# A bidirectional encoder on one core: the last two tiles of the attention branch's gate projection are queued behind the value matmuls of the last attention head

## The chip, the core and the metric

The kernel runs on one core of a Trainium2 chip. The metric is the time of one execution on the device in microseconds; lower is better. A core has engines that run side by side, each working through its own queue in order: the TensorE (PE in the profile; its weight loads are listed as PEld) for matmuls, the VectorE (DVE) for elementwise work and reductions, the ScalarE (ACT) for activation functions and casts, GpSimd (POOL), and SyncE (SP), which here issues the loads. Matmuls write to PSUM, everything else lies in SBUF.

## The reference

Two layers on 512 tokens of width 1024. Each layer normalizes its input, makes ten projections of it with one wide weight matrix `w_in`, runs two token mixers on them side by side (differential attention, and a gated linear recurrence in two directions), projects each mixer's output back to the model's width, gates both per channel and adds them, and projects the sum once more. Then follows a SwiGLU block.

```
h = rmsnorm(x, attn_norm[layer])
proj = h @ w_in[layer]
(a_q, a_k, a_v, b_q, b_ff, b_fb, b_i, b_g, gate_a, gate_b) = split_columns(proj)
y_a = diff_attention(a_q, a_k, a_v, ...) @ w_a[layer]        # 4 heads, values 128 wide
y_b = hgrn2_bidirectional(b_q, b_ff, b_fb, b_i, b_g, ...) @ w_b[layer]
merged = sigmoid(gate_a) * y_a + sigmoid(gate_b) * y_b
x = x + merged @ w_o[layer]
h = rmsnorm(x, ffn_norm[layer])
x = x + (silu(h @ w_gate[layer]) * (h @ w_up[layer])) @ w_down[layer]
```

In `diff_attention` each head has two softmax maps; the weights are the first less lambda times the second, and each head's output is normalized before it is joined with the others.

## The kernel before

**Numbers in two halves.** To keep the precision of float32, each operand of a large matmul is split into a rounded `hi` part and a rest `lo`, and each product is made of three matmuls (`mm3`: hi x hi, hi x lo, lo x hi), all adding into one PSUM bank. The rest `lo` x `lo` is left out. A split is one cast on ACT (the line of `ACT.copy` in `split_act`, L92) and one subtraction on DVE (recorded at L81).

**Projections.** `project_fm` (L214) makes a projection tile by tile. A tile is 128 output channels x 512 tokens. For each tile the weights are split (`wsplit`), then come 3 matmuls for each of the `k` chunks of the contraction (k = 8 for `w_in` and `w_o`, 24 matmuls; k = 4 for `w_a` and `w_b`, 12 matmuls), each with a 128x128 stationary weight block and 512 columns of the normalized input (`hh`, `hl`), then `evac`, which takes the bank to SBUF. Raw weights are loaded 1 MB at a time, which is two tiles with k = 8 and four with k = 4, into a pool of two buffers (`raw`). The split weights lie in a pool with three buffers for `hi` and three for `lo` (L102); a tile's buffers come free when its last matmul that reads them has ended. The accumulators take PSUM banks from a pool of four (`m`); the attention's small work has another four (`s`).

**Order.** The code is written for a framework that queues the instructions at build time. It keeps a priority by the order of the program text: at each point an engine gets the earliest instruction in the text that is ready in the framework's own reckoning. Loads, weight splits and evacuations stand in `with urgent():` blocks, which puts them ahead of everything that isn't urgent. So matmuls that come later in the text fill the places where earlier ones aren't ready. The order that comes out is fixed in each engine's queue. `behind(ins, other)` (L94) adds an edge of order alone: `ins` is queued after `other`, with no semaphore of its own.

**The mixer of one layer, from L726.** The recurrence's projections and its four heads come first. Then, from L790: the value projection; `attention` (L629); the second half of the gate of branch b (`gate_b(4)`, four tiles); the projection of branch b with `w_b`, eight tiles; the gate of branch a, eight tiles in two groups of four (columns from `G_A`, into `ga`), with a sigmoid of three ACT operations for each; then `w_a`, eight tiles (L815), and `w_o` (L821). `w_a` has the four heads as its four chunks, so every tile needs the output `oah`, `oal` of all heads, the last head in its last three matmuls. Its evacuation `merge` multiplies by `ga` and adds to `gb`.

**The attention.** For each of four heads `h` and each of four query blocks `t`: `exps` makes the scores (`qk`, four matmuls, L664 and L667), their negated row maximum (DVE, L669) and the exponentials with their row sums (ACT); `weights` joins the two maps on DVE (L674 to L677) into `e`; four transposes (`wt`, L714) turn them and `split_act` stores them as `wh` and `wl`. The loop is pipelined: the scores of the next block are made before the transposes of this one. When all four blocks of a head are turned, `values` (L679) multiplies them with the values: 12 matmuls into the bank `ao` (L210 to L212, L684 to L686). `finish` (L691) squares `ao`, sums the squares over the channels with two matmuls (`hss`, L406 and L409), scales, and splits the result into `oah` and `oal`. For the last head nothing of the attention follows, so its `values` and `finish` (L719) stand by themselves.

Of the kernel before, what the change touches and what calls it, by code (L numbers as in the profile page):

```python
# [18 lines left out]
P = 128  # L19
D = 1024  # L20
DC = D // P
T = 512
TC = T // P
LAYERS = 2
HEADS = 4
# [22 lines left out]
def kernel(  # L48
# [45 lines left out]
    def behind(ins, other):  # L94

        tc.add_manual_dep(ins.ins, other.ins.name,
                          mybir.DependencyInfo(mybir.DependencyClass.NoSync, mybir.DependencyReason.DATA),
                          reason="keep the tensor engine from waiting")
# [108 lines left out]
        return w[k0 * P:(k0 + nk) * P, c0:c0 + n].rearrange("(k p) c -> p k c", p=P)  # L207

    def mm3(ps, lh, ll, rh, rl, start, stop):
        PE.matmul(ps, lh, rh, start=start, stop=False)  # L210
        PE.matmul(ps, lh, rl, start=False, stop=False)  # L211
        PE.matmul(ps, ll, rh, start=False, stop=stop)  # L212

    def project_fm(w, cols, evac, k=DC, ah=None, al=None):  # L214

        ah = hh if ah is None else ah
        al = hl if al is None else al
        width = 2048 // k
        i = 0
        while i < len(cols):  # L220
            n = 1
            parts = ready.pop(cols[i], None)
            if parts is None:
                while n * P < width and i + n < len(cols) and cols[i + n] == cols[i] + n * P:
                    n += 1
                with urgent():
                    raw = wload(rows(w, 0, k, cols[i], n * P))
            for j in range(n):
                with urgent():
                    wh, wl = parts or wsplit(raw[:, :, j * P:(j + 1) * P])  # L230
                ps = mbank()
                for c in range(k):
                    mm3(ps, wh[:, c, :], wl[:, c, :], ah[:, c, :], al[:, c, :], c == 0, c == k - 1)
                with urgent():
                    evac(i + j, ps)
            i += n
# [157 lines left out]
    def head_squares(ps):  # L394
        sq = sm.tile([P, T], F32, tag="sq", name="hsq")
        act(sq, ps, AF.Square)
        sh = sm.tile([P, T], F32R, tag="sqh", name="sqh", bufs=1)
        sl = sm.tile([P, T], F32R, tag="sql", name="sql", bufs=1)
        first = ACT.copy(sh, sq)
        tt(sl, sq, sh.bitcast(F32), ALU.subtract)  # L400
        return (ps, sq, sh, sl), first
# [227 lines left out]
    def attention(l, aq, ak, avh, avl, oh, ol, ap):  # L629

        def operands(h):

            half = [slice(0, 64), slice(64, 128)]
            turned = []
            for src in (aq, ak):
                pt = bank("qkt")
                for t in range(TC):
                    PE.transpose(pt[:, t * P:(t + 1) * P], src[:, t, h * P:(h + 1) * P], ident)  # L640
                turned.append(pt)
            q2 = ap.tile([P, 2, T], F32R, tag="q2", name="q2", bufs=1)
            ka = ap.tile([P, 2, T], F32R, tag="ka", name="ka", bufs=1)
            kb = ap.tile([P, 2, T], F32R, tag="kb", name="kb", bufs=1)
            for pt, dst, swapped in ((turned[0], q2, None), (turned[1], ka, kb)):
                for c in range(2):
                    own, other = half[c], half[1 - c]
                    hi = dst[own, c, :]
                    ACT.copy(hi, pt[own, :])
                    mark = tt(dst[other, c, :], pt[own, :], hi.bitcast(F32), ALU.subtract)  # L650
                    if swapped is not None:
                        ACT.copy(swapped[other, c, :], pt[own, :])
                        mark = tt(swapped[own, c, :], pt[own, :], hi.bitcast(F32), ALU.subtract)
            return (q2, ka, kb), mark

        def exps(q2, ka, kb, t, mark):

            tok = slice(t * P, (t + 1) * P)
            nm = sm.tile([P, 2], F32, tag="nm", name="nm")
            den = sm.tile([P, 2], F32, tag="den", name="den")  # L660
            e = ap.tile([P, 2, T], F32, tag="e", name="e", bufs=2)
            ps = [bank("qk") for c in range(2)]
            for c in range(2):
                mm = PE.matmul(ps[c], q2[:, c, tok], ka[:, c, :], start=True, stop=False)  # L664
                if t == 0 and c == 0:
                    behind(mm, mark)
                PE.matmul(ps[c], q2[:, c, tok], kb[:, c, :], start=False, stop=True)  # L667
            for c in range(2):
                DVE.tensor_reduce(nm[:, c:c + 1], ps[c], AX.X, ALU.max, negate=True)  # L669
                mark = act(e[:, c, :], ps[c], AF.Exp, bias=nm[:, c:c + 1], accum=den[:, c:c + 1])  # L670
            return e, den, mark

        def weights(e, den):
            DVE.reciprocal(den, den)  # L674
            tt(den, den, dcoef[:, l, :], ALU.mult)
            tsc(e[:, 1, :], e[:, 1, :], den[:, 1:2], None, ALU.mult)
            return stt(e[:, 0, :], e[:, 0, :], den[:, 0:1], e[:, 1, :], ALU.mult, ALU.add)  # L677

        def values(h, wh, wl, mark):  # L679
            po = bank("ao")  # L680
            hc = slice(h * P, (h + 1) * P)
            for s in range(TC):
                if s == 0 and mark is not None:
                    behind(PE.matmul(po, avh[:, s, hc], wh[:, s, :], start=True, stop=False), mark)  # L684
                    PE.matmul(po, avh[:, s, hc], wl[:, s, :], start=False, stop=False)
                    PE.matmul(po, avl[:, s, hc], wh[:, s, :], start=False, stop=False)  # L686
                else:
                    mm3(po, avh[:, s, hc], avl[:, s, hc], wh[:, s, :], wl[:, s, :], s == 0, s == TC - 1)
            return head_squares(po)[0]

        def finish(h, parts, mark):  # L691
            o = head_norm(*parts, dgain[:, 4 * l + h:4 * l + h + 1], mark)
            split_act(o, oh[:, h, :], ol[:, h, :])

        todo = [(h, t) for h in range(HEADS) for t in range(TC)]
        ops, mark = operands(0)
        e, den, _ = exps(*ops, 0, mark)
        for n, (h, t) in enumerate(todo):
            mark = weights(e, den)
            if t == 0:  # L700
                if h:
                    parts = values(h - 1, wh, wl, mark)
                wh = ap.tile([P, TC, T], F32R, tag="wh", name="wh", bufs=1)
                wl = ap.tile([P, TC, T], F32R, tag="wl", name="wl", bufs=1)
            elif t == 1 and h:
                finish(h - 1, parts, mark)
            w, mark = e, None
            if n + 1 < len(todo):
                if t == TC - 1:
                    ops, mark = operands(h + 1)  # L710
                e, den, mark = exps(*ops, todo[n + 1][1], mark)
            pt = bank("wt")
            for s in range(TC):
                tr = PE.transpose(pt[:, s * P:(s + 1) * P], w[:, 0, s * P:(s + 1) * P], ident)  # L714
                if mark is not None:
                    behind(tr, mark)
            tok = slice(t * P, (t + 1) * P)
            split_act(pt.rearrange("p (s c) -> p s c", c=P), wh[:, :, tok], wl[:, :, tok])
        finish(HEADS - 1, values(HEADS - 1, wh, wl, None), None)  # L719


    last_silu = None
    for l in range(LAYERS):
        win = w_in[l]
        an = [vecs[:, V_FFN + 8 * l + c:V_FFN + 8 * l + c + 1] for c in range(DC)]
        with ExitStack() as mix:  # L726
# [10 lines left out]
            def scaled(dst):  # L737

                return lambda i, ps: tt(dst(i), ps, rbc, ALU.mult)
# [40 lines left out]
            with tc.tile_pool(name=f"merge{l}", bufs=1, reuse_waits="tile") as gm, ExitStack() as late:  # L780
# [11 lines left out]
                with tc.tile_pool(name=f"attn{l}", bufs=1, reuse_waits="tile") as ap:  # L792
                    rope(aq, ap)
                    rope(ak, ap)
                    attention(l, aq, ak, avh, avl, oah, oal, ap)
                    gate_b(4)
                    project_fm(w_b[l], [i * P for i in range(DC)],
                               lambda i, ps: tt(gb[:, i, :], gb[:, i, :], ps, ALU.mult),
                               k=4, ah=obh, al=obl)
                    ga = [gp.tile([P, HEADS, T], F32, tag=tag, name="ga") for tag in ("obh", "obl")]  # L800
                    for j in range(2):
                        project_fm(win, [G_A + (4 * j + i) * P for i in range(4)], scaled(lambda i: ga[j][:, i, :]))
                        for i in range(4):
                            sigmoid(ga[j][:, i, :])
                mp = late.enter_context(tc.tile_pool(name=f"mrg{l}", bufs=1, reuse_waits="tile"))
# [144 lines left out]
```

## Time and profile before

| what | value |
|---|---|
| median of three runs | 1627.63 us (1626.99 to 1627.94) |
| profiled execution | 1627.93 us |
| its span, first to last instruction | 1626.2 us |
| mean granted TensorE clock | 0.999 |
| PE busy | 1604.3 us, 99% of the span |
| PEld busy | 1323.7 us, 81% |
| DVE busy | 1010.8 us, 62% |
| ACT busy | 776.6 us, 48% |
| mean DMA traffic | 88 GB/s |

Rows of the profile's page and of the timeline name the line, the engine, the operation, and what is written and read by the program's own names (`m<-hh,hi`: a bank `m` from `hh` and `hi`). In the timeline the first two columns are the start from the beginning of the span and the duration, both in us; a bracket at the end gives the idle time of the engine ahead of the row and the instruction whose end released it. In the rows of a waits list stand the total in us, how many times, and the longest. A matmul's recorded duration holds a part that overlaps the next one, so it is the distance between starts that tells the rate. Because helpers record every call under one line, L210 to L212 are the three matmuls of every `mm3`, L81 is every DVE operation with two tensors, and L92 every cast of a split; the names tell them apart. `m<-hh` and `m<-hl` are projections of the layer's input, `m<-obh` is `w_b`, `m<-oah` and `m<-oal` are `w_a`, `m<-mh` and `m<-ml` are `w_o`. (In some rows the operands of a matmul are listed by the stationary one last.)

### The profile page before, as it was taken

The page shows a single profiled execution, that of the slowest core. Times are in us where ns is not written, and L with a number is a line of the kernel's source. Part 1 is how long each engine was busy: PE and PEld are TensorE (multiplying, and loading weights), DVE is VectorE, ACT ScalarE, POOL GpSimd, SP SyncE. Part 2 cuts the span into 40 slices and gives each one's busy share as a digit, 9 for nine tenths or more (in the row PEclk, how much of TensorE's full clock was granted, in tenths as well). Part 3 has the DMA queues.
Part 4 walks back from the last instruction along what each step waited for, and adds up shares of the span by engine and source line. Part 5 has one row for each costly group of instructions (what it writes and reads, how often), then busy time and mean ns, then how long its engine had stood idle before and what let it go on. Part 6 is the DMA issues. An engine that isn't in the chain of part 4 may idle for free.

```text
span 1626.2 us, 18701 instructions
## 1 busy us (share of the span) xinstructions
PE 1604.3 (99%) x7456; PEld 1323.7 (81%) x7456; DVE 1010.8 (62%) x1626; ACT 776.6 (48%) x1192; POOL 7.8 (0%) x21
## 2 busy tenths in 40 slices
PE   8999999999999999999999999999999999999998
PEld 6788888887888888888888888888878888888886
DVE  7878967887644444433368789788876444444224
ACT  5666675676433232322255567676754323233213
POOL 1000000000000000000000000000000000000000
PEclk9999999999999999999999999999999999999999
DMA  5212212221322233322332222122122233332321
GB/s 188 91 65 78 78 53 78 78 78 33 123 91 91 84 98 104 104 91 98 97 104 78 78 78 66 65 71 85 52 79 89 93 104 104 104 99 96 104 83 73
DMA packets 118823, 142.53 MB, mean 88 GB/s; under 512 B 3024, under 2 KB 101328, under 8 KB 118736
## 3 DMA queue, kind: packets, MB, share of 16 engines
q1 hardware_dynamic: 118592, 141.31, 26.8%
q8 instruction: 58, 0.95, 0.2%
q14 instruction: 29, 0.24, 0.0%
q10 hardware_dynamic: 144, 0.03, 0.0%
HBM read 139.23 MB, written 2.10 MB: 87 GB/s over the span
## 4 chain that ended last, share of the span: by engine, by line
PE 85%; DVE 9%; ACT 4%; issue 1%; DMA 0%; SPq 0%; ACTq 0%
PE m L210 24%; PE m L212 24%; PE m L211 24%; DVE fl L81 2%; DVE lo L81 2%; PE sc L551 2%; PE s L212 1%; PE s L211 1%; PE s L210 1%; PE qk L667 1%; DVE z L81 1%; PE wt L714 1%; PE po L601 1%; PE qk L664 1%; ACT hi L92 1%
## 5 line engine op out<-in xcount | busy, mean ns | idle before, releaser
L92 ACT CAST hi<-raw 128x1024 fp32r<-128x1024 f32 (+2 forms) x280 | 276.6, 989 | 612.2 <-PE m L211 469.5
L210 PE MATMUL m<-hh,hi 128*128 128x512 f32 x1216 | 476.7, 392 | 7.1 <-ACT hh L78 7.1
L211 PE MATMUL m<-hl,hi 128*128 128x512 f32 x1216 | 476.1, 392 | 0.1
L212 PE MATMUL m<-hh,lo 128*128 128x512 f32 x1216 | 476.2, 392 | 0.0
L81 DVE TENSOR_TENSOR lo<-raw,hi 128x1024 fp32r<-128x1024 f32 (+2 forms) x280 | 320.3, 1145 | 184.8 <-ACT hi L92 183.6
L210 PEld LDWEIGHTS m<-hh,hi 128*128 128x128 f32 x1216 | 229.2, 188 | 54.6 <-ACT hh L78 7.9
L211 PEld LDWEIGHTS m<-hl,hi 128*128 128x128 f32 x1216 | 228.9, 188 | 48.0 <-DVE hl L84 1.4
L212 PEld LDWEIGHTS m<-hh,lo 128*128 128x128 f32 x1216 | 229.1, 188 | 47.1
L81 DVE TENSOR_TENSOR gu<-m,rbc 128x512 f32<-128x512 f32 x88 | 60.9, 692 | 241.0 <-PE m L212 237.0
L210 PE MATMUL m<-hi,hh 128*128 128x512 f32 x256 | 101.5, 396 | 0.0
L211 PE MATMUL m<-lo,hh 128*128 128x512 f32 x256 | 100.9, 394 | 0.0
L212 PE MATMUL m<-hi,hl 128*128 128x512 f32 x256 | 100.8, 394 | 0.0
L78 ACT ACTIVATE fl<-fl 128x1024 f32<-128x1024 f32 (+1 forms) x56 | 48.4, 872 | 43.8 <-DVE fl L81 43.8
L210 PE MATMUL m<-gh,hi 128*128 128x512 f32 x176 | 68.5, 389 | 0.0
L211 PE MATMUL m<-gl,hi 128*128 128x512 f32 x176 | 68.5, 389 | 0.0
L212 PE MATMUL m<-gh,lo 128*128 128x512 f32 x176 | 68.5, 389 | 0.0
L212 PEld LDWEIGHTS m<-hi,hl 128*128 128x128 f32 x256 | 48.1, 188 | 9.6
L211 PEld LDWEIGHTS m<-lo,hh 128*128 128x128 f32 x256 | 48.2, 188 | 9.4
L210 PEld LDWEIGHTS m<-hi,hh 128*128 128x128 f32 x256 | 48.1, 188 | 9.3
L551 PEld LDWEIGHTS sc<-fl 128*128 128x128 f32 x384 | 49.0, 191 | 7.1 <-DVE fl L81 2.7
L551 PE MATMUL sc<-fl 128*128 128x128 f32 x384 | 51.4, 277 | 1.6 <-DVE fl L81 1.5
L211 PE MATMUL m<-ml,hi 128*128 128x512 f32 x128 | 49.7, 391 | 0.0
(254 smaller groups left out, 2334.3 us busy)
## 6 DMA issues: line engine op xcount, KB each, us to landing
raw<-in_w_in_dram SPq DMA_DIRECT2D x47, 1024.0 KB, 5.0
raw<-in_w_gate_dram SPq DMA_DIRECT2D x22, 1024.0 KB, 5.1
raw<-in_w_up_dram SPq DMA_DIRECT2D x22, 1024.0 KB, 5.1
raw<-in_w_down_dram SPq DMA_DIRECT2D x19, 1024.0 KB, 5.0
raw<-in_w_o_dram SPq DMA_DIRECT2D x8, 1024.0 KB, 5.0
raw<-in_w_b_dram SPq DMA_DIRECT2D x4, 1024.0 KB, 5.0
raw<-in_w_a_dram SPq DMA_DIRECT2D x4, 1024.0 KB, 4.9
raw<-in_w_down_dram SPq DMA_DIRECT2D x4, 768.0 KB, 4.3
```

The costliest lines, as they stand in the source:

```text
L78: return ACT.activation(o, i, func, **kw)
L81: return DVE.tensor_tensor(o, a, b, op)
L92: return ACT.copy(hi, src), tt(lo, src, hi.bitcast(F32), ALU.subtract)
L210: PE.matmul(ps, lh, rh, start=start, stop=False)
L211: PE.matmul(ps, lh, rl, start=False, stop=False)
L212: PE.matmul(ps, ll, rh, start=False, stop=stop)
L551: mm = PE.matmul(ps[:, c], K[:, c], Q[:, c], start=True, stop=True)
L601: mm = PE.matmul(po[:, tok], a, b, start=i == 0, stop=i == len(terms) - 1)
L664: mm = PE.matmul(ps[c], q2[:, c, tok], ka[:, c, :], start=True, stop=False)
L667: PE.matmul(ps[c], q2[:, c, tok], kb[:, c, :], start=False, stop=True)
L714: tr = PE.transpose(pt[:, s * P:(s + 1) * P], w[:, 0, s * P:(s + 1) * P], ident)
```

## The change

`mm3` returns its first and last matmul, and `attention` returns the last matmul of the last head's `values`. `project_fm` gets two arguments: for the last `kept` tiles of its list, the first matmul is queued behind the instruction `after`. The gate projection of branch a uses it in its second group of four tiles (`kept=2*j` with j = 1): the tiles 2 and 3 of that group, which are the last two of the eight, are queued behind the last value matmul. Loads, splits, evacuations and sigmoids carry no such edge.

```
     def mm3(ps, lh, ll, rh, rl, start, stop):
-        PE.matmul(ps, lh, rh, start=start, stop=False)
+        first = PE.matmul(ps, lh, rh, start=start, stop=False)
         PE.matmul(ps, lh, rl, start=False, stop=False)
-        PE.matmul(ps, ll, rh, start=False, stop=stop)
+        return first, PE.matmul(ps, ll, rh, start=False, stop=stop)
...
-    def project_fm(w, cols, evac, k=DC, ah=None, al=None):
+    def project_fm(w, cols, evac, k=DC, ah=None, al=None, kept=0, after=None):
...
                 for c in range(k):
-                    mm3(ps, wh[:, c, :], wl[:, c, :], ah[:, c, :], al[:, c, :], c == 0, c == k - 1)
+                    mm, _ = mm3(ps, wh[:, c, :], wl[:, c, :], ah[:, c, :], al[:, c, :], c == 0, c == k - 1)
+                    if c == 0 and i + j >= len(cols) - kept:
+                        behind(mm, after)
...
-                    mm3(po, avh[:, s, hc], avl[:, s, hc], wh[:, s, :], wl[:, s, :], s == 0, s == TC - 1)
-            return head_squares(po)[0]
+                    _, last = mm3(po, avh[:, s, hc], avl[:, s, hc], wh[:, s, :], wl[:, s, :], s == 0, s == TC - 1)
+            return head_squares(po)[0], last
...
-        finish(HEADS - 1, values(HEADS - 1, wh, wl, None), None)
+        parts, last = values(HEADS - 1, wh, wl, None)
+        finish(HEADS - 1, parts, None)
+        return last
...
-                    attention(l, aq, ak, avh, avl, oah, oal, ap)
+                    last = attention(l, aq, ak, avh, avl, oah, oal, ap)
...
                     for j in range(2):
-                        project_fm(win, [G_A + (4 * j + i) * P for i in range(4)], scaled(lambda i: ga[j][:, i, :]))
+                        project_fm(win, [G_A + (4 * j + i) * P for i in range(4)], scaled(lambda i: ga[j][:, i, :]),
+                                   kept=2 * j, after=last)
```

The other call of `values` takes the first of the two results.

More of the change, by code (lines that the diff above doesn't have):

```diff
@@ L701, in attention @@
                 if h:
-                    parts = values(h - 1, wh, wl, mark)
+                    parts, _ = values(h - 1, wh, wl, mark)
                 wh = ap.tile([P, TC, T], F32R, tag="wh", name="wh", bufs=1)
```

## The prediction

> **What bounds the kernel now.** First the page: busy time by engine and the shares of the chain that ended last; then the whole list of what the TensorE waits for.
>
> ```profile
> span 1626.2 us, 18701 instructions
> PE 1604.3 (99%) x7456; PEld 1323.7 (81%) x7456; DVE 1010.8 (62%) x1626; ACT 776.6 (48%) x1192; POOL 7.8 (0%) x21
> PE 85%; DVE 9%; ACT 4%; issue 1%; DMA 0%; SPq 0%; ACTq 0%
> PE m L210 <- ACT oah L92: 1.2, 2, 0.6
> PE m L212 <- DVE lo L81: 1.7, 2, 0.9
> ```
>
> The TensorE works from end to end. The last two rows are the only long waits inside a layer, once in each of the two layers: the w_a projection stands still for the last head's `oah`, and soon after for a `lo` half of its own weights. Their sum, 2.9 us of 1626, is what a reordering aims at. So the question is what the reordering takes from the stretch before. I read the tail of the attention in layer 0, then three windows: the tail, the w_a stretch behind it, and 40 us of plain matmuls as a yardstick.
>
> ```profile
> 367.60 0.39 PE L212 MATMUL m<-hh,lo 128*128 128x512 f32 x1
> 367.82 0.39 PE L210 MATMUL m<-hh,hi 128*128 128x512 f32 x1
> ...
> 382.37 0.63 PE L714 MATMUL wt<-ident,e 128*128 128x128 f32 x4
> 382.75 0.48 PE L212 MATMUL m<-hh,lo 128*128 128x512 f32 x1
> ...
> 383.76 0.42 PE L210 MATMUL ao<-wh,avh 128*128 128x512 f32 x1
> ...
> 385.41 0.40 PE L211 MATMUL ao<-wl,avh 128*128 128x512 f32 x1
> ...
> 387.73 0.39 PE L212 MATMUL ao<-wh,avl 128*128 128x512 f32 x1
> ...
> 393.56 0.97 PE L210 MATMUL m<-oah,hi 128*128 128x512 f32 x3 [0.59 <-ACT oah L92]
> ...
> 398.19 0.49 PE L212 MATMUL m<-oah,lo 128*128 128x512 f32 x1 [0.85 <-DVE lo L81]
> ...
> 410.58 0.39 PE L210 MATMUL m<-mh,hi 128*128 128x512 f32 x1
> ```
>
> ```profile
> 367.80:387.95 20.15, 20.15 (x96) 16.24 (x95) 15.69 (x31) 15.43 (x31) 0.00 (x0) 1.00 0.00 0
> 387.95:410.58 22.63, 21.19 (x91) 16.30 (x89) 17.47 (x27) 11.56 (x18) 0.00 (x0) 1.00 0.29 93
> 500.00:540.00 40.00, 40.00 (x178) 33.12 (x177) 19.11 (x23) 12.04 (x15) 0.00 (x0) 1.00 0.34 106
> ```
>
> The columns are the window, its length, then busy time and count of PE, weight loads, DVE, ACT, POOL, the granted clock and DMA. The pitch of a 512-column matmul is 40.00 / 177 = 0.226 us. I call A the moment at which the last `ao` matmul is through: 387.73 + 0.22 = 387.95. Up to A the TensorE is busy 20.15 of 20.15 us. What keeps it so is filler: matmuls of later projections, issued wherever the last head's chain (qk, maximum, exp, weights, transposes) isn't ready. Which filler it was:
>
> ```profile
> L211 PE MATMUL m<-oal,hi 128*128 128x512 f32 x32 | 12.5, 391 | 0.0
> L212 PE MATMUL m<-hh,lo 128*128 128x512 f32 x17 | 6.7, 396 | 0.0
> L211 PE MATMUL m<-hl,hi 128*128 128x512 f32 x16 | 6.4, 397 | 0.0
> L210 PE MATMUL m<-hh,hi 128*128 128x512 f32 x16 | 6.3, 397 | 0.0
> ```
>
> These are groups between 367.82 and 410.5. The gate projection has 16+16+16 = 48 matmuls here (one of the 17 is the row at 367.60, still under way): exactly two tiles of 8x3. So the tiles that the change moves, which I call T6 and T7, ran from 367.82 to 382.75, all of it ahead of A. The w_a projection has 3x32 = 96.
>
> **The change part by part.** Its operations are the same ones; no DMA, cast or matmul is added or taken away, and no semaphore wait either, since the new edge is one of order on the TensorE alone (`behind`). The return values cost nothing. Only the first matmul of T6 and of T7 is tied, but the others accumulate behind it, so 48 matmuls go from before A to behind it, in each layer.
>
> *Behind A* they cost 48 x 0.226 = 10.85 us of TensorE time that was before A until now.
>
> *Before A*, what takes their place? Nothing with `hh` is left: T6 and T7 are the last of the filler. Next in program order is w_a, whose heads 0 to 2 are ready before A. But its weights must first be split into `hi` and `lo`, and that pool has three buffers. The casts of `hi`, on ACT:
>
> ```profile
> 351.62 1.05 ACT L92 CAST hi<-raw 128x1024 fp32r<-128x1024 f32 x1 [0.49 <-PE m L211]
> ...
> 357.08 1.06 ACT L92 CAST hi<-raw 128x1024 fp32r<-128x1024 f32 x1 [0.51 <-PE m L211]
> ...
> 364.16 0.62 ACT L92 CAST hi<-raw 128x512 fp32r<-128x512 f32 x1 [1.27 <-PE m L211]
> ...
> 377.03 0.61 ACT L92 CAST hi<-raw 128x512 fp32r<-128x512 f32 x1
> ...
> 382.47 0.62 ACT L92 CAST hi<-raw 128x512 fp32r<-128x512 f32 x1 [0.57 <-PE m L211]
> ```
>
> A 128x1024 cast is a gate tile, a 128x512 one a w_a tile. Each waits until a matmul of an older tile gives its buffer back. T6 is split at 351.62 and T7 at 357.08, long before use, as splits are urgent and ask for no matmul of their own tile; the first w_a tile takes the third buffer at 364.16. All this is ahead of 367.82, the first instruction that the change holds back, so I expect it unchanged. The second and third w_a tile (377.03, 382.47) got the buffers of T6 and T7 as these ended. With T6 and T7 kept until A, these two casts fall behind A too. What can fill before A is one w_a tile with three heads, 9 matmuls, and the trace of before has 9 of w_a before A already (3 between the rows at 382.75 and 383.76, 6 between the `ao` at 383.76 and that at 385.41). So nothing new comes in: 10.85 us of slots stay empty, less what A comes earlier.
>
> *How much earlier A comes.* The attention goes ahead of the filler by program order, so the filler costs it mostly what it takes on DVE (one row of ACT stands among these):
>
> ```profile
> 376.83 0.68 DVE L81 TENSOR_TENSOR ga<-m,rbc 128x512 f32<-128x512 f32 x1
> ...
> 378.03 0.68 DVE L81 TENSOR_TENSOR lo<-raw,hi 128x512 fp32r<-128x512 f32 x1
> 378.63 0.48 DVE L88 TENSOR_SCALAR e<-e,den 128x512 f32<-128x512 f32 x1
> ...
> 383.03 0.59 ACT L92 CAST wh<-wt 128x512 fp32r<-128x512 f32 x1
> 383.27 0.69 DVE L81 TENSOR_TENSOR ga<-m,rbc 128x512 f32<-128x512 f32 x1 [0.44 <-PE m L212]
> 383.88 0.68 DVE L81 TENSOR_TENSOR lo<-raw,hi 128x512 fp32r<-128x512 f32 x1
> 384.47 0.68 DVE L81 TENSOR_TENSOR wl<-wt,wh 128x512 fp32r<-128x512 f32 x1
> ```
>
> T6's evacuation and the second w_a split stand in the line ahead of the weights, at 0.60 us each (378.03 to 378.63): 1.2 us. T7's evacuation and the third split, 1.2 us at 383.27 to 384.47, hold up the last `wl`, for which `ao` waits at 385.41; of that 0.85 goes, as `wl` still has to wait for its own `wh` (383.03 + 0.59 = 383.62). And transposes and qk matmuls no longer queue behind filler of a full TensorE: I take 0.5 us of the few tenths at each step. Together 2.55 us, A at 385.4. From one side: nothing (A at 387.95, if ACT or the banks hold the chain as before). From the other: DVE has 15.69 us of work in the window 367.80 to 387.95; without the four operations (4 x 0.68 = 2.7) 13.0 remain, so the last `wl` can't end before 380.8, and with eleven `ao` matmuls behind it (2.5) and 0.2 to start A isn't before 383.5: 4.45 us earlier at most.
>
> *What is saved behind A.* In the window 387.95 to 410.58 there are 96 - 9 = 87 w_a matmuls and two `hss`: 89 x 0.226 = 20.1 of 22.63 us, so 2.5 us are lost, 1.44 of them in the two waits. After the change T6 and T7 cover the last head's chain (A to the row at 393.56: 5.6 us, against 10.85) and the splits follow one by one; I take all 2.45, with 1.44 as the lower end. The sigmoids of T6 and T7, now behind A, are due only for the merge of w_a's tiles 6 and 7, six tiles x 12 x 0.226 = 16 us later: nothing. Should that cover fail, three ACT operations a tile would stand in the merge, about 2 us.
>
> *Sum for a layer:* 10.85 - 2.55 - 2.45 = +5.85 us; from 10.85 - 4.45 - 2.45 = +4.0 to 10.85 - 0 - 1.44 = +9.4. Layer 1 has the same waits at the same lengths (the "2" in the waits), so twice: +11.7, from +8 to +18.8. The profiled execution took 1627.93 us (1.7 around the span), 0.3 above the median 1627.63 of the three runs. I forecast 1627.9 + 11.7 = 1640 with the rounding; alone this case has 1636 to 1647.
>
> **The rivals.**
>
> *The clock falls in the thinned tail.* Between 367.80 and A the TensorE would have 20.15 - 10.85 = 9.3 us of work in 17.6. The trace bounds what a cold array costs, by the start of the kernel, and shows when the grant falls, at its end:
>
> ```profile
> 10.00:15.00 5.00, 5.00 (x13) 3.81 (x13) 4.36 (x7) 4.95 (x10) 0.00 (x0) 1.00 0.98 332
> 15.00:20.00 5.00, 5.00 (x23) 4.12 (x23) 4.08 (x8) 2.12 (x4) 0.00 (x0) 1.00 0.86 270
> 1618.80 0.39 PE L212 MATMUL s<-hi,gl 128*128 128x512 f32 x1
> 1620.00:1627.00 7.00, 0.00 (x0) 0.00 (x0) 1.60 (x4) 1.94 (x5) 0.00 (x0) 0.67 0.28 109
> ```
>
> In the first stretch 13 matmuls pass where 22 to 23 do later (the grant column shows no figure under 1.00 there, so I go by the counts): nine lost, 9 x 0.226 = 2.0 us. Behind the last matmul (1618.80) the mean grant of 0.67 over 7 us would be a fall to a half 2.4 us into that window, some 3 us after the work ended. One such fall a layer makes +7.9 instead of +5.85: 1644, and up to 1649 with A unmoved. Against it: transposes, qk and the 9 w_a matmuls break the tail up, and by the distances of the chain's steps I estimate no hole over 2 us. [...]
>
> *The w_a tiles step in.* If T6's and T7's splits came after those of the second and third w_a tile, 27 matmuls could fill instead of 9: 18 x 0.226 = 4.1 us better, +1.8 a layer, 1631.5; with A at its earliest 1628, no change. The ACT casts at 351.62 and 357.08 speak against it.
>
> *The other side: the tail is held by T6 and T7 themselves.* If A came earlier by the whole 10.85, only the saving would be left: 1627.9 - 4.9 = 1623. It decides at 10.85 - 2.45 = 8.4 us, A at 379.5; the 13.0 us of DVE work say no.
>
> *The edge does nothing* (the order stays): 1628. The first matmul of T6 stands 20 us ahead of A in the queue, so the edge must move it.
>
> **How the numbers follow.** Main case 70%, clock 17%, w_a steps in 6% (half of it within 0.2%), early tail 4%, no effect 3%. 0.2% (3.3 us) is about what a measurement here can tell from no change. Faster 0.05, same 0.06, slower 0.89. The range 1634 to 1648 takes in the main case's bounds and most of the clock's, and leaves out the other three.
>
> **What would show it.** Right: no gate matmul with `hh` between the end of the tile ahead of T6 (367.6) and the last `ao`; a run of 48 behind it; PE busy well under 20 of 20 us in the tail, at about half; the second w_a cast of `hi` behind A; the waits for `oah` and `lo` in w_a gone; A about 2.5 us earlier; the first `mh` matmul near 416.5. Wrong: casts of several w_a tiles before A, A before 380, or a granted clock under 1.00 near 375 to 395.

## The result, and the profile after

The changed kernel takes 1649.05 us (median of four runs) against 1627.79 for the kernel before, measured beside it: a ratio of 1.0131, interval 1.0119 to 1.0142. It is 21.3 us slower, where 11.7 were forecast and 1634 to 1648 was the range: the right sign, the right place, and nearly half of the cost missing. The page of the profiled execution:

```profile
span 1647.8 us, 18695 instructions
PE 1614.3 (98%) x7456; PEld 1330.9 (81%) x7456; DVE 1012.3 (61%) x1626; ACT 776.8 (47%) x1192; POOL 7.7 (0%) x21
PEclk9999999998999999999999999999899999999999
```

The same operations on every engine, 21.6 us more of span, and the granted clock under nine tenths in two slices, those of the two attention tails. The list of what the TensorE waits for has lost both waits in w_a. In their place stand waits inside the attention, for the transposes `wt`, the square sums `hss` and the first `ao` matmul:

```profile
PE wt L717 <- ACT e L78: 6.3, 2, 3.4
PE wt L717 <- DVE e L84: 2.6, 4, 0.8
PE hss L412 <- DVE sql L81: 2.2, 2, 1.1
PE ao L210 <- ACT wh L92: 1.4, 2, 0.7
```

The timeline of the TensorE in the tail of layer 0, from the last filler matmul with `hh` to the first matmul of w_o:

```profile
367.81 0.40 PE L212 MATMUL m<-hh,lo 128*128 128x512 f32 x1
...
378.90 1.09 PE L717 MATMUL wt<-ident,e 128*128 128x128 f32 x4 [3.41 <-ACT e L78]
...
382.51 0.80 PE L210 MATMUL ao<-wh,avh 128*128 128x512 f32 x1 [0.68 <-ACT wh L92]
...
384.25 0.63 PE L210 MATMUL ao<-wh,avh 128*128 128x512 f32 x1
384.68 0.63 PE L211 MATMUL ao<-wl,avh 128*128 128x512 f32 x1
...
387.53 0.40 PE L212 MATMUL ao<-wh,avl 128*128 128x512 f32 x1
387.76 0.39 PE L210 MATMUL m<-hh,hi 128*128 128x512 f32 x1
...
399.43 0.39 PE L210 MATMUL m<-oah,hi 128*128 128x512 f32 x1
...
421.19 0.39 PE L210 MATMUL m<-mh,hi 128*128 128x512 f32 x1
```

Between 367.81 and 387.76 there is no projection matmul at all, and a hole of 3.41 us. The `ao` matmuls start 0.43 us apart (384.25, 384.68), not 0.227. The first matmul of w_a comes at 399.43, behind the whole of T6 and T7. Two windows, from the last filler matmul to A and from A to the first matmul of w_o, and the groups in the second one:

```profile
367.81:387.76 19.95, 12.02 (x40) 7.87 (x39) 13.49 (x27) 10.65 (x23) 0.00 (x0) 0.74 0.00 1
387.76:421.19 33.43, 33.43 (x147) 27.26 (x146) 21.82 (x33) 16.84 (x26) 0.00 (x0) 1.00 0.20 63
```

```profile
L212 PE MATMUL m<-oah,lo 128*128 128x512 f32 x32 | 12.5, 389 | 0.0
L210 PE MATMUL m<-oah,hi 128*128 128x512 f32 x32 | 12.5, 389 | 0.0
L211 PE MATMUL m<-oal,hi 128*128 128x512 f32 x32 | 12.5, 389 | 0.0
L212 PE MATMUL m<-hh,lo 128*128 128x512 f32 x16 | 6.2, 389 | 0.0
```

The attention's end, A, is at 387.76, 19.95 us behind the last filler; before it was 387.95, 20.35 behind. So A gained 0.4 us, and the TensorE worked 12.02 of 19.95 us instead of all. Behind A lie 48 + 96 + 2 matmuls in 33.43 us without a wait; before it were 89 in 22.63 us. With A 0.4 us earlier, layer 0 costs 33.43 - 22.63 - 0.4 = 10.4 us; layer 1, between the same two places, 11.0. That is the whole 21.

What the forecast said of the buffers is there as well. The casts of `hi`:

```profile
351.86 1.05 ACT L92 CAST hi<-raw 128x1024 fp32r<-128x1024 f32 x1 [0.49 <-PE m L211]
...
357.31 1.06 ACT L92 CAST hi<-raw 128x1024 fp32r<-128x1024 f32 x1 [0.51 <-PE m L211]
...
364.38 0.62 ACT L92 CAST hi<-raw 128x512 fp32r<-128x512 f32 x1 [1.26 <-PE m L211]
...
393.96 0.62 ACT L92 CAST hi<-raw 128x512 fp32r<-128x512 f32 x1 [0.65 <-PE m L211]
```

T6, T7 and one w_a tile are split as early as before, and the second w_a tile waits for T6's buffer until 393.96. But the first w_a tile didn't run ahead of A, and it wasn't its split that held it. DVE:

```profile
368.76 0.68 DVE L81 TENSOR_TENSOR ga<-m,rbc 128x512 f32<-128x512 f32 x1
369.36 0.68 DVE L81 TENSOR_TENSOR lo<-raw,hi 128x512 fp32r<-128x512 f32 x1
```

The second row ends its split, at 370.04. The first is the evacuation of the gate tile ahead of T6: behind it no tile holds a bank of the pool `m` until T6 begins at 387.76.

### The profile page after: what moved, and what is told of

Its sections match the earlier page's. It is cut to its first block, busy times and chain, and to the rows that moved or that the text cites. A ratio compares the mean times of both kernels' runs of the same rounds, so it can differ in the third digit from the quotient of the medians.

```text
span 1647.8 us, 18695 instructions
## 1 busy us (share of the span) xinstructions
PE 1614.3 (98%) x7456; PEld 1330.9 (81%) x7456; DVE 1012.3 (61%) x1626; ACT 776.8 (47%) x1192; POOL 7.7 (0%) x21
## 4 chain that ended last, share of the span: by engine, by line
PE 84%; DVE 10%; ACT 4%; issue 1%; DMA 0%; SPq 0%; ACTq 0%; DVEq 0%
PE m L211 24%; PE m L210 24%; PE m L212 24%; DVE fl L81 2%; DVE lo L81 2%; PE sc L554 2%; PE s L212 1%; PE s L210 1%; PE s L211 1%; DVE z L81 1%; PE po L604 1%; PE qk L670 1%; PE wt L717 1%; ACT hi L92 1%; PE qk L667 1%
## 5 line engine op out<-in xcount | busy, mean ns | idle before, releaser
L78 ACT ACTIVATE e<-qk,nm 128x512 f32<-128x512 f32 x64 | 43.5, 683 | 14.3 <-DVE nm L672 14.1
```

What stands on the lines that cost most here:

```text
L78: return ACT.activation(o, i, func, **kw)
```

## The experiments

Two things departed from the forecast: no w_a matmul fills the tail, and the TensorE's clock falls in it. The first four kernels take them apart.

**e1_bank_claimed: the kept tiles take their banks early.** `mm3` returns its second matmul as the one to be tied, so that the first of each kept tile runs as filler.

```
     def mm3(ps, lh, ll, rh, rl, start, stop):
-        first = PE.matmul(ps, lh, rh, start=start, stop=False)
-        PE.matmul(ps, lh, rl, start=False, stop=False)
-        return first, PE.matmul(ps, ll, rh, start=False, stop=stop)
+        PE.matmul(ps, lh, rh, start=start, stop=False)
+        second = PE.matmul(ps, lh, rl, start=False, stop=False)
+        return second, PE.matmul(ps, ll, rh, start=False, stop=stop)
```

> The edge is put on the second matmul of each kept tile instead of the first, so that the first one runs early and takes the tile's PSUM bank. Theory (banks of one pool are handed out in the order of the text, so a kept tile without a bank holds back every w_a tile): the first w_a tile's 9 matmuls for heads 0 to 2, and the 2 of the kept tiles, run before the last value matmul; 11 x 0.227 = 2.5 us a layer come back, so 1649 - 5 = 1644 if the clock falls as in the changed kernel, and down to 1638 if the thicker tail keeps it at full. Rival (w_a waits before that moment for something else, its split or the heads): no w_a matmul ahead of the last value matmul, 1648.

Measured: 1643.28 us, ratio 1.0093 (1.0079 to 1.0106). Groups of its TensorE between 366.15 and its A at 386.81:

```profile
L211 PE MATMUL m<-oal,hi 128*128 128x512 f32 x3 | 1.6, 527 | 0.7 <-DVE oal L81 0.7
L212 PE MATMUL m<-oah,lo 128*128 128x512 f32 x3 | 1.5, 507 | 0.5 <-DVE lo L81 0.5
L210 PE MATMUL m<-oah,hi 128*128 128x512 f32 x3 | 1.3, 431 | 0.5 <-ACT oah L92 0.5
```

Three times three: the 9 matmuls of w_a run ahead once the kept tiles have their banks, and from A to w_o it takes 30.93 us instead of 33.43. So it was the held first matmul of T6 and T7 that kept w_a out. I read it as a matter of banks: with none given to T6 and T7, the w_a tile, which stands behind them in the text, got none either, although all four were empty. That it is the bank, and nothing else that hangs on the first matmul, no run takes apart. Of 5.8 us saved, 2 x 2.5 are the nine and the two first matmuls of the kept tiles.

The clock still fell, for 10.2 us in each layer, though with w_a's matmuls in it no hole of this tail is over 0.83 us. The steps of the clock ahead of the two falls and the first one behind:

```profile
372.52:375.93 3.41, 2.04 (x8) 0.89 (x6) 3.12 (x8) 3.32 (x9) 0.00 (x0) 1.00 0.00 0
375.93:379.35 3.42, 2.33 (x6) 1.21 (x6) 3.13 (x8) 0.95 (x4) 0.00 (x0) 0.50 0.00 0
1181.48:1184.89 3.41, 1.91 (x7) 0.80 (x5) 3.12 (x8) 3.23 (x9) 0.00 (x0) 1.00 0.00 0
```

**e2_warm: the change with idle work in the holes.** Ahead of the kept tiles, 48 matmuls go into a bank that nobody reads.

```
+                if kept and i + j == len(cols) - kept:
+                    dummy = mbank()
+                    for c in range(24 * kept):
+                        PE.matmul(dummy, ah[:, c % k, :P], ah[:, (c + 1) % k, :], start=True, stop=True)
                 ps = mbank()
```

> The change as it is, with 48 matmuls per layer added whose result nobody reads, as filler in the places that the two kept tiles left. Theory (the half clock makes the last value matmuls late): the granted clock stays at 1.00 through the attention's end, the twelve value matmuls take 2.7 us instead of 5.25, the last one ends about 2 us earlier than in the kernel before since two evacuations and two splits less stand in DVE's queue, and the rest behind it is as in the changed kernel: some 8.5 us a layer over the kernel before, 1645, so faster than the changed kernel although it does more. Rival (the value matmuls are held by the chain on DVE and ACT, the clock costs nothing): 1649 or more.

Measured: 1645.18 us, ratio 1.0104 (1.0090 to 1.0118): with 96 matmuls more than the changed kernel it is about 4 us faster. Its two windows, and two neighbouring `ao` matmuls:

```profile
367.44:386.54 19.10, 19.10 (x93) 15.35 (x91) 13.74 (x27) 11.34 (x24) 0.00 (x0) 1.00 0.00 0
386.54:419.93 33.39, 33.39 (x147) 27.26 (x146) 21.81 (x33) 16.85 (x26) 0.00 (x0) 1.00 0.19 64
```

```profile
384.49 0.39 PE L210 MATMUL ao<-wh,avh 128*128 128x512 f32 x1
384.72 0.39 PE L211 MATMUL ao<-wl,avh 128*128 128x512 f32 x1
```

The clock stays at 1.00, the `ao` matmuls are 0.23 apart, and the twelve take 3.24 us (with two of the idle matmuls among them) against 5.25 and 5.52 in the two layers of the changed kernel. The way to the first `ao` takes as long in both (15.85 us against 15.61 and 15.95 from the first `qk` of the last head's second block), so nearly all of the clock's price fell on these twelve matmuls.

**e3_one_kept: only T7 is kept.**

```
-                                   kept=2 * j, after=last)
+                                   kept=j, after=last)
```

> Only the last tile of the gate projection is kept behind, not two. Sum by the same terms for a layer: 24 matmuls x 0.227 = 5.4 go behind, 9 of w_a (2.0) can't run ahead, the stalls of 2.1 go, the last value matmul comes 0.85 earlier: +4.5, so 1637 with a full clock. If the clock falls in the shorter thin stretch as well, 2 to 3 us a layer more: 1642. Rival (the cost goes with the number of kept tiles alone): half of the changed kernel's 21.3, 1638.4 with the clock falling half as long.

Measured: 1640.88 us, ratio 1.0077 (1.0063 to 1.0091), so 12.5 us for one tile a layer against 21.3 for two. From A to w_o 27.99 us, 5.36 more than before, as the sum had it (5.4 + 2.0 - 2.1). The rest lies ahead of A: it comes 0.6 us later than before in layer 0 and 1.6 in layer 1 (21.90 and 22.80 us from that `qk`, against 21.26 and 21.19), where 0.85 earlier was expected, with the clock at half for 6.8 and 10.2 us. The 1642 with a falling clock was 1 us too high. The time alone doesn't rule out the rival: half of the changed kernel's cost is a ratio of 1.0065, just inside the interval.

**e11_claimed_warm: both departures undone.** e1's early first matmul, and 36 idle matmuls as in e2.

> The changed kernel with both departures from the forecast undone: the kept tiles claim their banks with an early first matmul (w_a's 9 matmuls run ahead, as forecast), and 36 matmuls whose result nobody reads keep the clock up. Theory (these two are all that separates 1649 from the forecast of 1640): 30.9 us from the last value matmul to w_o, value matmuls in 3.2 us or less, granted clock 1.00, +6.0 us a layer over the kernel before, 1640. Rival (a third term is missing): over 1642.

Measured: 1639.78 us, ratio 1.0075 (1.0062 to 1.0087), beside 1627.87 for the kernel before. Its two windows:

```profile
365.60:384.75 19.15, 19.15 (x92) 15.16 (x90) 13.75 (x27) 11.34 (x24) 0.00 (x0) 1.00 0.00 0
384.75:415.65 30.90, 30.90 (x137) 25.19 (x135) 21.64 (x33) 16.87 (x26) 0.00 (x0) 1.00 0.21 68
```

That is the forecast of 1640, with w_a's nine matmuls ahead of A and a clock at 1.00, and it is closer than the terms deserve: two of the 48 matmuls run ahead here as well (0.45 us a layer less), and against that A gains 0.4 us less than forecast and 0.3 less is saved behind it. A layer costs 30.90 - 22.63 - 2.11 = 6.16 us, where 5.85 were forecast. Nothing larger is missing beside the two.

The other four ask what would have covered the last head's chain without emptying the tail.

**e8_wa_pairs: more w_a tiles in the same buffers, and nothing kept.** A w_a tile fills half of a split buffer. Here two tiles are split at once (`m` is 2 for w_a and 1 for all others).

```
...
-                with urgent():
-                    wh, wl = parts or wsplit(raw[:, :, j * P:(j + 1) * P])
+                if parts is not None:
+                    wh, wl = parts
+                elif j % m == 0:
+                    with urgent():
+                        wh, wl = wsplit(raw[:, :, j * P:(j + m) * P])
+                col = slice(j % m * P, (j % m + 1) * P)
...
```

> The kernel before, with no tile kept behind; instead w_a's weights are split for two tiles at a time, which fills a buffer of the split pool instead of half of one. Theory (the stalls in w_a come from having three split w_a tiles, so 27 matmuls without the last head, where the banks would allow four tiles, 36): nine more matmuls cover the last head's chain, 2.0 of the 2.45 us lost a layer come back, 1627.8 - 4.2 = 1623.5, and both waits leave the list. Rival (the last head's chain is late by itself and what is gained is lost again in the merges): 1627.8, no change.

Measured: 1628.64 us, ratio 1.0003 (0.9994 to 1.0012): no change. The tail did what the theory said, the waits for `oah` and `lo` are gone, and from that `qk` to w_o it takes 42.00 us instead of 43.89. But the list of waits has a new row:

```profile
PE m L211 <- DVE ml L81: 3.2, 2, 1.6
```

Four tiles now wait for the last head, get it together, and hand DVE four merges at once; w_o then stands 1.6 us a layer for a `ml` half. The rival's words fit: gained, and lost again in the merges.

**e10_pairs_interleaved: w_o asks later for the last chunk.** e8 with the first two tiles of w_o side by side.

```
...
+                ps = [mbank(), mbank()]
+                for c in range(DC):
+                    for j in range(2):
+                        wh, wl = two[j]
+                        mm3(ps[j], wh[:, c, :], wl[:, c, :], mh[:, c, :], ml[:, c, :], c == 0, c == DC - 1)
...
-                project_fm(w_o[l], [i * P for i in range(DC)], residual, ah=mh, al=ml)
+                project_fm(w_o[l], [i * P for i in range(2, DC)], lambda i, ps: residual(i + 2, ps), ah=mh, al=ml)
```

> w_a's weights split for two tiles at a time (as in e8_wa_pairs), and the first two tiles of w_o run chunk by chunk side by side, so that the last chunk of the merged input is asked for 42 matmuls after w_a's end instead of 21. Theory (e8_wa_pairs gained 1.9 us a layer in w_a and gave 1.6 to 2 back waiting for the last ml half, as DVE gets the merges of four tiles at once): the wait for ml goes, and 1628.3 - 2 x 1.9 = 1624.5 remains. Rival (DVE is simply short of time from w_a to the norm behind w_o): the wait moves on to a later place and the time stays at 1628.

Measured: 1623.61 us beside 1627.87, ratio 0.9974 (0.9966 to 0.9983). This is the one version here that is faster than the kernel before, by 4.3 us. The head of its list of waits has neither `oah` nor `lo` nor `ml`:

```profile
PE m L210 <- ACT hh L78: 6.2, 2, 5.8
PE st L508 <- ACT kt L503: 2.0, 1, 2.0
PE sc L555 <- DVE fl L81: 1.6, 3, 1.1
```

**e12_interleaved_only: its control.** The same w_o on the kernel before.

> The kernel before with nothing changed but the first two tiles of w_o side by side: the control of e10_pairs_interleaved. In the kernel before no wait for ml is on the list, so both theories expect no change, 1628; if it gains by itself, the gain of e10_pairs_interleaved isn't due to the pairs.

Measured: 1628.16 us, ratio 1.0001 (0.9992 to 1.0010). The interleaving alone gives nothing, so it takes the pair.

**e10b_pairs_pool: another way to relieve DVE.** e8 with the merge's addition as `POOL.tensor_tensor`.

> w_a's weights split for two tiles at a time, and the addition of each merge given to GpSimd, which takes eight of the 0.6 us operations a layer from DVE. Theory (DVE's backlog of merges is what e8_wa_pairs waits for): the wait for ml shrinks, 1625 to 1627, if GpSimd's addition takes less than the 2.7 us of a w_a tile. Rival (GpSimd's own time, of which this trace shows nothing, is longer than that): slower than e8_wa_pairs, 1630 or more.

Measured: 1637.15 us, ratio 1.0056 (1.0041 to 1.0072), slower. The group of these additions, and the wait for what follows them:

```profile
L816 POOL TENSOR_TENSOR gb<-gb,ga 128x512 f32<-128x512 f32 x16 | 29.6, 1866 | 1184.8 <-DVE ga L81 1184.8
PE m L210 <- ACT mh L92: 7.1, 4, 2.8
```

GpSimd takes 1.87 us for an addition that DVE does in 0.68. That is under the 2.7 us of a w_a tile, and w_o waits for `mh` all the same. Ahead of the last two additions of layer 0 GpSimd itself stands idle:

```profile
410.32 1.68 POOL L816 TENSOR_TENSOR gb<-gb,ga 128x512 f32<-128x512 f32 x1 [1.23 <-DVE ga L81]
414.05 2.17 POOL L816 TENSOR_TENSOR gb<-gb,ga 128x512 f32<-128x512 f32 x1 [2.05 <-DVE ga L81]
```

DVE makes a tile's `ga` only behind the `ml` of the tile before (for the last tile at 413.29, behind an `ml` at 412.68), that `ml` waits for `mh`, and `mh` for GpSimd's addition. So the last tiles go through DVE, GpSimd and ACT one at a time, 3.7 us apart. In these holes the clock falls as well, to half for 6.8 us in each layer, and how much of the 9.3 us is its part wasn't taken apart. The condition that I gave for a gain was the wrong one.

## Why the prediction was right or wrong

*48 matmuls go behind A:* right, term for term. The second window holds them, and 146 matmuls at 0.227 leave 0.3 us of 33.43.

*The buffers:* right. T6, T7 and one w_a tile were split at the forecast places, the second w_a tile behind A.

*"What can fill before A is one w_a tile with three heads, 9 matmuls":* this step failed. None did. The nine then stand behind A, 9 x 0.227 = 2.0 us a layer, 4.1 in all. I had counted the split buffers and left out the other pool that a tile needs, the PSUM banks. As I read it, a tile further on in the text doesn't overtake one that has no bank yet. e1 shows that letting the first matmul of the kept tiles through is enough; by which rule of the framework it is so, no trace shows.

*How much earlier A comes:* the mechanism was right, but the clock took the gain. The last `wl` on DVE starts at 382.49; 384.47 - 1.2 - 0.85 = 382.4 was the forecast. With the clock up, A comes 2.1 to 2.2 us earlier (e2, e11: 19.1 us from that `qk` against 21.26 before) where 2.55 were taken. In the changed kernel the half clock ate all but 0.4 us in layer 0, and in layer 1 A came 0.3 later than before.

*What is saved behind A:* 2.1 us of the 2.45; the chain was covered, as forecast.

*The clock, put at nothing in the main sum:* this is the second step that failed. As a rival it had 17% and 2.0 us a layer. It came, in both layers, at about 2 us each (changed kernel less e2: 4 us), and a granted clock under 1.00 near 375 to 395 was named as a sign of being wrong. Two things in the reasoning were wrong. "I estimate no hole over 2 us" was wrong: the third `wt` waited 3.41 us, since nothing stood between the last `qk` and the transposes once w_a didn't run. And the question whether a hole exceeds a length was the wrong one. The trace of before has a single fall, 3.2 us behind its last matmul, and doesn't show that shorter holes leave the clock up; in e1 w_a's nine matmuls fill the tail as forecast, no hole is over 0.83 us, and the clock falls in both layers. So this step would have failed without the other.

The account: 1640, and 4.1 for the nine matmuls, and about 4 for the clock, make 1648; the last 1 us is about what the two other terms fell short by, 0.4 us a layer for A and 0.3 behind it. e11 takes the two large ones away and gives 1639.8. That the prediction also has a 1649, for the clock with A unmoved, is luck: it counts the clock's 2.0 us and the lost lead of A, 2.55, as two losses, which were one, and nothing for w_a. The rival with w_a stepping in, the early tail and the edge without effect didn't come.

## What to carry to other kernels

A matmul that fills a hole is worth its place there; before queueing it later, name what fills the hole instead, and go through every pool that this work needs (split buffers and PSUM banks alike), because a tile whose first matmul is held back can hold back all that stand behind it. Where the TensorE will run thin for a few microseconds, reckon with a half clock on the first dense work behind it (about 2 us each time in the changed kernel), even if no single hole is long (0.83 us at most in e1, where it fell behind steps with 2.04 and 1.91 us of work in 3.41). Where a stall lies behind one chain, more work that doesn't depend on the chain may cover it (here two tiles in one buffer), but look at what gets the burst when the chain ends.

## What the runs showed of the hardware

The clock falls and rises in steps of 3.41 us: at half for 10.24 and 17.07 us in the two layers of the changed kernel (three and five steps), for 6.8 and 10.2 in e3, for 10.2 twice in e1. The two falls of the changed kernel and the one at its end, at 1643.45, lie 236 and 135 such steps apart (805.5 and 460.8 us, 3.413 each). Steps of that length around the falls, at 377.13 in layer 0 and at 1182.65 in layer 1 (columns as before; the granted clock is the figure behind POOL's):

```profile
366.90:370.31 3.41, 2.25 (x11) 1.44 (x9) 2.75 (x5) 3.17 (x8) 0.00 (x0) 1.00 0.00 0
370.31:373.72 3.41, 2.07 (x9) 1.28 (x9) 3.30 (x8) 3.25 (x6) 0.00 (x0) 1.00 0.00 0
373.72:377.13 3.41, 1.20 (x4) 0.62 (x4) 3.12 (x8) 2.96 (x8) 0.00 (x0) 1.00 0.02 5
377.13:380.55 3.42, 1.09 (x4) 0.71 (x4) 3.13 (x7) 1.31 (x3) 0.00 (x0) 0.50 0.00 0
...
383.96:387.37 3.41, 3.41 (x10) 2.63 (x9) 0.00 (x0) 0.00 (x0) 0.00 (x0) 0.50 0.00 0
387.37:390.79 3.42, 3.42 (x16) 2.40 (x14) 0.69 (x1) 1.48 (x3) 0.00 (x0) 1.00 0.00 0
```

```profile
1179.24:1182.65 3.41, 1.85 (x9) 1.14 (x8) 3.41 (x7) 3.38 (x8) 0.00 (x0) 1.00 0.00 0
1182.65:1186.07 3.42, 3.00 (x9) 1.74 (x9) 3.32 (x8) 3.29 (x7) 0.00 (x0) 0.50 0.00 0
```

In layer 1 the grant fell behind a step in which the TensorE was busy for 1.85 of 3.41 us, with no hole over 1.1 us; in e1 it fell behind steps with 2.04 and 1.91, with no hole over 0.7 us. In layer 0 it stayed up behind steps with 2.25 and 2.07 and fell behind one with 1.20. So a thin step can be enough, and it needn't be an idle one. But the recorded busy time doesn't draw the line. In the kernel before, with the steps counted back from the fall at its end, 1622.4, the grant stays at 1.00 behind a step in the recurrence with 1.68:

```profile
79.58:82.99 3.41, 1.68 (x15) 1.68 (x16) 2.63 (x8) 1.90 (x4) 0.00 (x0) 1.00 0.93 295
82.99:86.41 3.42, 3.42 (x24) 3.03 (x23) 2.45 (x8) 1.38 (x2) 0.00 (x0) 1.00 0.02 7
```

At the same place in e8 and e12 it fell, for one step, behind 1.46 and 1.45. What does draw the line stays open. In the changed kernel the grant rose again behind a step of unbroken matmuls at half rate (3.41 of 3.41 us busy, from 383.96 and from 1196.31). Where the steps begin was different in each of four runs: 1.1 us behind a whole number of steps from the start of the span in the kernel before, 1.6 in the changed kernel, 0.5 in e1, 2.4 in e3. That fits layer 1 staying at half for two steps more than layer 0 with the same queue: the fall comes 9.3 us behind the start of the last filler in layer 0 (367.81) and 3.4 in layer 1 (1179.25).
